# Values and output gate of three of four token blocks as seven block products with sums kept in PSUM

## The chip, the cores and the metric

The kernel runs on one core of one Trainium2 chip. The metric is the device time of one execution in microseconds (us); lower is better. TensorE multiplies, VectorE and ScalarE work on elements, GpSimd does a power now and then, and SyncE (SP) issues the DMA transfers.

## What is computed

One decoder layer on 2048 tokens of width 1024, in fp32. The part that the change touches is the combined input projection and what hangs on it:

```python
n = rms_norm(h, norm1_w)
z = n @ w_in            # columns: queries 256, keys 256, values 512, low rank 16, output gate 512, spatial u 512, spatial v 512
# A: gated linear attention, 4 heads (key 64, value 128 wide), chunks of 64 tokens
S_t = diag(alpha_t) S_{t-1} + k_t^T v_t ;  o_t = q_t S_t
A = rms_norm(o, gla_norm_w) * silu(gate)
# B: spatial gating, chunks of 128 tokens
B = u * (tril(W_s) @ layer_norm(v) + b)
h = h + concat([A, B]) @ w_out
h = h + (silu(m @ w_ffn_gate) * (m @ w_ffn_up)) @ w_ffn_down     # m = rms_norm(h)
out = rms_norm(h)
```

## The kernel before

The tokens are worked off in four blocks of 512 (`NB`); in the text they are the first to the fourth block, in the code `blk` 0 to 3. A loop `s` over two pairs runs `mix` and `project` (output projection) for two blocks, then gate and up (`gate_up`) and the down-projection (`down`) for both. Gate, up and down already run as seven block products of Winograd's form, with sums of blocks of `w_d` that a background generator, `down_sums` (L322 to L337, 11 jobs), writes to the DRAM tensor `td` during the first two blocks.

Every fp32 product is three fp32r matmuls (`mm3`, L112 to L116): each operand is split into a high part that ScalarE copies (L94) and a low part that VectorE subtracts (L95), 12 significant bits each. A weight tile (`load_w`, L101) is a load of 512 KB to a `raw` buffer (3 of them), the copy `whi` and the subtraction `wlo` (4 pairs in flight).

```python
def split(hi, lo, src):
    nc.scalar.copy(hi, src)
    nc.vector.tensor_tensor(lo, src, f32(hi), ALU.subtract)
```

Work that is no dense product is written as generators. `start` puts one into a list, and `tick` runs one step of each; `tok_group`, `col_pair` and the others call `tick` after each weight tile's matmuls. `finish` runs a generator to its end. Within that written order a scheduler sets the order of each engine's instructions, and each engine works its own in order. PSUM has 8 banks, one per `ps` tile.

In `mix` (L342) a block goes through: the first half of the gating values with the low rank columns; the decay; keys; queries; values (`tok_group` over the 512 value columns: 4 tiles of 24 matmuls, drained by ScalarE, L438), from which four DMAs (L442) bring the values into the halves of `right` that other rows hold; `chunks()` (L446), started when the values are there, in four steps of two chunks each. A step is 16 matmuls for the states' increments (L453), 8 updates of the state on VectorE (L462), 16 matmuls for the scores (L469) and 2 masked copies (L473). It runs in the ticks of the second half of the gating values (L483) and of the output gate (L510: again 4 tiles of 24 matmuls, drained by `gate_done`, ScalarE's Silu and a scale on VectorE, L506 and L508). `sv_norm` (L486) is the layer norm of the gating values, with GpSimd's power in between. Then `attend` (L517) runs in the ticks of the spatial gate's products (`gate_pair` with two tiles of `su` each, L551 to L573).

Of the kernel before, what the change touches and what calls it, by code (L numbers as in the profile page):

```python
# [8 lines left out]
F32 = mybir.dt.float32  # L9
# [24 lines left out]
def hybrid_block(ctx, tc, x, norm1_w, w_in, w_gate_up, b_gate_up, gla_norm_w, sg_ln_w, sg_ln_b,  # L34
# [28 lines left out]
    # A generator emits one step at a time; tick() runs a step of each after a weight tile's products.  # L63
# [37 lines left out]
    def load_w(srcs, a, b):  # L101
        """srcs: DRAM views [P, a, ...], side by side; the two parts of [P, a, b] in SBUF."""
# [9 lines left out]
    def mm3(o, l, r, first, last):  # L112
        (lh, ll), (rh, rl) = l, r
        nc.tensor.matmul(o, lhsT=ll, rhs=rh, start=first, stop=False)  # L114
        nc.tensor.matmul(o, lhsT=lh, rhs=rl, start=False, stop=False)  # L115
        nc.tensor.matmul(o, lhsT=lh, rhs=rh, start=False, stop=last)  # L116

    def rsq(dst, ss, n, k):
        """dst = 1 / sqrt(ss / n + eps)"""
# [10 lines left out]
    class Act:  # L130
        """A transposed operand: nk row tiles of 128 by 512 tokens, two parts."""
# [10 lines left out]
        def row(self, k, n=1):  # L142
            """Row tiles k .. k+n-1, for all tokens."""
# [3 lines left out]
        def put(self, i, t, src):  # L147
            """Row tiles 4i .. 4i+3 of token tile t from PSUM."""
            s = slice(t * P, (t + 1) * P)
            split(self.hi[i][:, :, s], self.lo[i][:, :, s], src.rearrange("p (a b) -> p a b", b=P))  # L150

    def row_tiles(u):
        """Two units as four row tiles of D."""
# [37 lines left out]
    def tok_group(w, col_list, act, ks=2, order=None, outer=None, done=None, before=None, ws=None, hook=None, pre=None):  # L191
        """Token-major product: four PSUM tiles [128 tokens, n]."""
# [39 lines left out]
    def col_pair(ws, act, a=0, b=NB):  # L232
        """Transposed product: two PSUM tiles [128 columns, tokens a..b]."""
# [23 lines left out]
    # 0 where a chunk starts, 1 elsewhere: the prefix scan's carry  # L257
# [3 lines left out]
    # keep[j, i] = 1 where j <= i, in both halves of the rows  # L261
# [10 lines left out]
    bd = dram.tile([2, P, 4, NB], F32, name="bd")  # L272

    # the decay's up-projection: rows hi, hi, lo against the low-rank input's hi, lo, hi
# [9 lines left out]
    def constants():  # L284
# [9 lines left out]
        # spatial gating: masked, transposed weights and the two biases  # L294
# [27 lines left out]
    def down_sums():  # L322
# [672 lines left out]
```

## Time and profile before

| | |
|---|---|
| runs, us | 2015.26, 2015.6, 2017.57 |
| median, us | 2015.6 |
| span of the profiled execution, us | 2014.3 |
| TensorE busy, us | 1987.2 (99%) |
| VectorE busy, us | 1422.5 (71%) |
| ScalarE busy, us | 858.8 (43%) |
| DMA engines busy | 45.2% |

The times are of whole executions. The profile is of one execution more, taken by the hardware profiler; its own time is its span, from the first instruction to the last. L95 is line 95 of the kernel. An engine is busy while an instruction of it runs; matmuls are pipelined, so a matmul's duration overlaps that of the next, and what one costs is read from the distance of starts. The granted clock is TensorE's, as a share of the full 2.4 GHz.

### The profile page before, as it was taken

The page shows a single profiled execution, that of the slowest core. Times are in us where ns is not written, and L with a number is a line of the kernel's source. Part 1 is how long each engine was busy: PE and PEld are TensorE (multiplying, and loading weights), DVE is VectorE, ACT ScalarE, POOL GpSimd, SP SyncE. Part 2 cuts the span into 40 slices and gives each one's busy share as a digit, 9 for nine tenths or more (in the row PEclk, how much of TensorE's full clock was granted, in tenths as well). Part 3 has the DMA queues.
Part 4 walks back from the last instruction along what each step waited for, and adds up shares of the span by engine and source line. Part 5 has one row for each costly group of instructions (what it writes and reads, how often), then busy time and mean ns, then how long its engine had stood idle before and what let it go on. Part 6 is the DMA issues. An engine that isn't in the chain of part 4 may idle for free. (4 is left out here: it accounts for less than half of the span.)

```text
span 2014.3 us, 26324 instructions
## 1 busy us (share of the span) xinstructions
PE 1987.2 (99%) x9909; PEld 1659.1 (82%) x9909; DVE 1422.5 (71%) x2397; ACT 858.8 (43%) x1418; POOL 80.8 (4%) x102
## 2 busy tenths in 40 slices
PE   7999999999999999999999999999999999999998
PEld 6888888878888888888888888887888888888886
DVE  5676776798777777555776655658977877775466
ACT  4534635453333333433562535346433333334334
POOL 1011000000000000000100100100000000000000
PEclk9999999999999999999999999999999999999999
DMA  5646664323323324865754344323332332367555
GB/s 192 188 168 222 228 200 167 115 94 105 115 95 102 118 95 145 290 200 185 242 178 105 115 143 144 103 84 116 114 111 95 106 114 95 104 208 268 188 164 197
DMA packets 189790, 303.05 MB, mean 150 GB/s; under 512 B 14503, under 2 KB 93021, under 8 KB 188638
## 3 DMA queue, kind: packets, MB, share of 16 engines
q1 hardware_dynamic: 189662, 301.36, 45.2%
q8 instruction: 78, 1.28, 0.3%
q14 instruction: 50, 0.41, 0.1%
HBM read 224.25 MB, written 72.88 MB: 148 GB/s over the span
## 5 line engine op out<-in xcount | busy, mean ns | idle before, releaser
L94 ACT CAST whi<-raw 128x1024 fp32r<-128x1024 f32 (+3 forms) x191 | 192.0, 1006 | 403.3 <-PE ps L115 208.5
L95 DVE TENSOR_TENSOR wlo<-raw,whi 128x1024 fp32r<-128x1024 f32 (+3 forms) x191 | 221.9, 1168 | 150.1 <-ACT whi L94 144.1
L114 PE MATMUL ps<-whi,aop 128*128 128x512 f32 x552 | 215.1, 390 | 0.0
L116 PE MATMUL ps<-whi,aop 128*128 128x512 f32 x552 | 214.8, 389 | 0.0
L115 PE MATMUL ps<-wlo,aop 128*128 128x512 f32 x552 | 214.8, 389 | 0.0
L94 ACT CAST op<-sw 128x512 fp32r<-128x512 f32 x176 | 107.5, 621 | 184.5 <-DVE sw L634 159.6
L114 PE MATMUL ps<-whi,nTl 128*128 128x512 f32 (+2 forms) x512 | 177.4, 346 | 3.4 <-DVE nTl L95 3.4
L116 PE MATMUL ps<-whi,nTh 128*128 128x512 f32 (+2 forms) x512 | 174.4, 341 | 0.0
L115 PE MATMUL ps<-wlo,nTh 128*128 128x512 f32 (+2 forms) x512 | 174.3, 340 | 0.0
L95 DVE TENSOR_TENSOR aop<-raw,aop 128x1024 fp32r<-128x1024 f32 x84 | 95.3, 1135 | 97.5 <-ACT aop L94 97.3
L95 DVE TENSOR_TENSOR op<-sw,op 128x512 fp32r<-128x512 f32 x176 | 121.5, 692 | 43.0 <-ACT op L94 42.6
L94 ACT CAST aop<-raw 128x1024 fp32r<-128x1024 f32 x84 | 82.0, 979 | 136.6 <-DMA raw<-ad 135.1
L116 PEld LDWEIGHTS ps<-whi,aop 128*128 128x128 f32 x552 | 103.6, 188 | 21.6
L115 PEld LDWEIGHTS ps<-wlo,aop 128*128 128x128 f32 x552 | 103.6, 188 | 21.4
L114 PEld LDWEIGHTS ps<-whi,aop 128*128 128x128 f32 x552 | 103.6, 188 | 21.4
L659 ACT COPY p<-ps 128x512 f32<-128x512 f32 x88 | 51.5, 588 | 149.2 <-PE ps L116 143.6
L95 DVE TENSOR_TENSOR op<-raw,op 128x512 fp32r<-128x512 f32 x132 | 89.3, 693 | 31.0 <-ACT op L94 30.5
L114 PEld LDWEIGHTS ps<-whi,nTl 128*128 128x128 f32 x512 | 98.1, 192 | 14.5 <-ACT whi L94 3.5
L116 PEld LDWEIGHTS ps<-whi,nTh 128*128 128x128 f32 x512 | 98.1, 192 | 10.2
L115 PEld LDWEIGHTS ps<-wlo,nTh 128*128 128x128 f32 x512 | 98.2, 192 | 9.4
L114 PE MATMUL ps<-whi,mixTl 128*128 128x512 f32 x256 | 101.9, 398 | 1.4 <-DVE mixTl L95 1.2
L114 PE MATMUL ps<-nTh,wlo 128*128 128x512 f32 x256 | 101.8, 398 | 0.0
(229 smaller groups left out, 4712.4 us busy)
## 6 DMA issues: line engine op xcount, KB each, us to landing
raw<-in_w_in_dram SPq DMA_DIRECT2D x72, 512.0 KB, 3.9
raw<-ad SPq DMA_DIRECT2D x70, 512.0 KB, 3.9
raw<-in_w_ffn_gate_dram SPq DMA_DIRECT2D x44, 512.0 KB, 3.6
raw<-in_w_ffn_up_dram SPq DMA_DIRECT2D x44, 512.0 KB, 3.6
raw<-td SPq DMA_DIRECT2D x40, 512.0 KB, 3.9
ad<-cg SPq DMA_DIRECT2D x66, 256.0 KB, 2.0
ad<-cs SPq DMA_DIRECT2D x22, 768.0 KB, 3.6
raw<-in_w_out_dram SPq DMA_DIRECT2D x32, 512.0 KB, 3.8
```

Source lines behind the costliest of these rows:

```text
L94: nc.scalar.copy(hi, src)
L95: nc.vector.tensor_tensor(lo, src, f32(hi), ALU.subtract)
L114: nc.tensor.matmul(o, lhsT=ll, rhs=rh, start=first, stop=False)
L115: nc.tensor.matmul(o, lhsT=lh, rhs=rl, start=False, stop=False)
L116: nc.tensor.matmul(o, lhsT=lh, rhs=rh, start=False, stop=last)
L659: nc.scalar.copy(t[m], o)
```

## The change

For the second to the fourth block values and output gate are one product: 512 tokens x 1024 by 1024 x 1024 columns, quartered by halves of the tokens, of the inner dimension and of the columns (values, gate). It is done in seven block products of 256 x 512 by 512 x 512 (`pair_product`), each with two weight tiles of 12 matmuls, in the order 1, 2, 7, 6, 4, 5, 3. The running sums stay in three pairs of PSUM banks: products 1, 6, 5, 3 add into one, 7 and 4 into another. `drain` reads a sum after a product: 1, 2, 6 and 4 give the values, 7, 5 and 3 the gate.

Four left operands are sums of quarters of the block's normed tokens (`Halves`, made in ticks of the stages before the product), four right operands are sums of quarters of `w_in`, which `weight_sums` (formerly `down_sums`, now 15 jobs, each in place in one buffer) writes to the DRAM tensor `vd`. The second half of the gating values now comes ahead of the product, and the chunk steps start after product 4. `mix` also loads its block's x rows anew (`hx`) at the start of `attend`. The first block is as before.

```diff
+    class Halves:
...
+            a, b, c = spare
+            whole(a, 0, 0)
+            whole(b, 1, 0)
+            nc.vector.tensor_tensor(c, a, b, ALU.subtract)
+            put(7, c)
+            yield
+            whole(c, 1, 1)
+            nc.vector.tensor_tensor(c, c, b, ALU.add)
+            put(5, c)
+            yield
...
+    def pair_product(load, left, order, bank, drain):
+
+        acc = {}
+        for m in order:
+            key = bank[m]
+            first = key not in acc
+            if first:
+                acc[key] = [ps(), ps()]
+            for kk in range(2):
+                hi, lo = load(m, kk)
+                for th in range(2):
+                    for j in range(2):
+                        mm3(acc[key][th], left(m, 2 * kk + j, th), (hi[:, j, :], lo[:, j, :]),
+                            first and kk + j == 0, kk + j == 2, True)
+                    if kk:
+                        drain(m, th, acc[key][th])
+                tick()
...
-        for j in range(NF // 2):
-            raw, t = bigt(F32, "wdraw"), bigt(F32, "wdt")
...
+        jobs = [(blocks(w_in, (k, 4 + k), (C_V, C_GOUT)), vd[:, k]) for k in range(4)]
+        jobs += [(blocks(w_d, (2 * j, 2 * j + 1), (0, 512)), td[:, j]) for j in range(NF // 2)]
         for _ in range(8):
             yield
+        for srcs, dst in jobs:
+            t = bigt(F32, "wsum")
+            for i, src in enumerate(srcs):
+                nc.sync.dma_start(t[:, i], src)
+            b11, b12, b21, b22 = (t[:, i] for i in range(4))
+            nc.vector.tensor_tensor(b11, b12, b11, ALU.subtract)
+            nc.vector.tensor_tensor(b12, b22, b12, ALU.subtract)
+            nc.vector.tensor_tensor(b22, b22, b11, ALU.subtract)
+            nc.vector.tensor_tensor(b21, b21, b22, ALU.subtract)
+            nc.sync.dma_start(dst.rearrange("m p d -> p m d"), t)
             for _ in range(4):
                 yield
...
+        if halves is None:
+            tok_group(w_in, [(C_V, 512)], nT, done=lambda t, acc: nc.scalar.copy(v[:, t, :], acc))
+            g_chunks = chunks_start()
+            second_half()
...
+            tok_group(w_in, [(C_GOUT, 512)], nT, done=gate_done)
+        else:
+            second_half()
+            g_svn = start(sv_norm())
+            finish(g_half)
...
+            def drain(m, th, acc):
+                lo, hi = th, 2 + th
+                if m == 1:
+                    nc.scalar.copy(v[:, lo, :], acc)
+                elif m == 2:
+                    nc.vector.tensor_tensor(v[:, lo, :], acc, v[:, lo, :], ALU.add)
+                elif m == 7:
+                    nc.scalar.copy(gw[:, hi, :], acc)
+                elif m == 6:
+                    nc.scalar.copy(v[:, hi, :], acc)
+                elif m == 4:
+                    nc.vector.tensor_tensor(v[:, hi, :], acc, v[:, hi, :], ALU.add)
+                    if th:
+                        started.append(chunks_start())
+                elif m == 5:
+                    nc.vector.tensor_tensor(gw[:, hi, :], acc, gw[:, hi, :], ALU.add)
+                    nc.scalar.activation(gw[:, hi, :], gw[:, hi, :], AF.Silu)
+                    gate_scale(hi)
+                else:
+                    gate_done(lo, acc)
+
+            pair_product(load, halves, (1, 2, 7, 6, 4, 5, 3), {1: 0, 6: 0, 5: 0, 3: 0, 2: 1, 7: 2, 4: 2}, drain)
...
+        hx = dma_x(x2, blk)
```

Before, VectorE in the third block from the third chunk step to the second tile of the spatial gate (`rs`, `sv`: layer norm of the gating values; `wlo`: low part of a weight tile; `right`, `state`: the state's updates; `left`: the masked copy of the scores; `gw`: the gate's scale):

```order
L462 SCALAR_TENSOR_TENSOR right_8774<-right_8773,dec,ps 64x128 x4
L462 SCALAR_TENSOR_TENSOR right_8773<-right_8774,dec,ps 64x128 x4
L473 COPY_PREDICATED left<-keep,ps 64x2x128 x2
L120 TENSOR_SCALAR rs<-mv 128x4
L95 TENSOR_TENSOR wlo<-raw,whi 128x1024
L497 TENSOR_SCALAR sv<-sv,mv,rs 128x128 x4
L462 SCALAR_TENSOR_TENSOR right_8774<-right_8773,dec,ps 64x128 x4
L462 SCALAR_TENSOR_TENSOR state<-right_8774,dec,ps 64x128 x4
L473 COPY_PREDICATED left<-keep,ps 64x2x128 x2
L95 TENSOR_TENSOR wlo<-raw,whi 128x1024 x2
L508 TENSOR_TENSOR gw<-gw,gnw 128x512 x3
L95 TENSOR_TENSOR wlo<-raw,whi 128x1024
```

Between two chunk steps there is a weight split, and the spatial gate's first splits stand ahead of the gate's scales.

With the change, VectorE in the third block from the last values' adds (L620 behind product 4) into the third chunk step (L536 and L547 are the steps' updates and masked copies, L624 is the gate's add behind product 5, L581 its scale):

```order
L620 TENSOR_TENSOR v<-ps,v 128x512 x2
L95 TENSOR_TENSOR wlo<-raw,whi 128x1024
L536 SCALAR_TENSOR_TENSOR right_8900<-right_8899,dec,ps 64x128 x4
L536 SCALAR_TENSOR_TENSOR right_8899<-right_8900,dec,ps 64x128 x4
L547 COPY_PREDICATED left<-keep,ps 64x2x128 x2
L536 SCALAR_TENSOR_TENSOR right_8900<-right_8899,dec,ps 64x128 x4
L536 SCALAR_TENSOR_TENSOR right_8899<-right_8900,dec,ps 64x128 x4
L547 COPY_PREDICATED left<-keep,ps 64x2x128 x2
L624 TENSOR_TENSOR gw<-ps,gw 128x512 x2
L536 SCALAR_TENSOR_TENSOR right_8900<-right_8899,dec,ps 64x128 x4
L536 SCALAR_TENSOR_TENSOR right_8899<-right_8900,dec,ps 64x128
L581 TENSOR_TENSOR gw<-gw,gnw 128x512 x2
```

The one split here is that of product 3's second tile; the first two steps stand one behind the other. The same queue goes on, to the spatial gate:

```order
L536 SCALAR_TENSOR_TENSOR right_8899<-right_8900,dec,ps 64x128 x3
L547 COPY_PREDICATED left<-keep,ps 64x2x128 x2
L536 SCALAR_TENSOR_TENSOR right_8900<-right_8899,dec,ps 64x128 x4
L536 SCALAR_TENSOR_TENSOR state<-right_8900,dec,ps 64x128 x4
L547 COPY_PREDICATED left<-keep,ps 64x2x128 x2
L581 TENSOR_TENSOR gw<-gw,gnw 128x512 x2
L95 TENSOR_TENSOR wlo<-raw,whi 128x1024 x5
```

The split of the spatial gate's first tile is the first of the last five, behind all steps and the scales of product 3's gate. In the fourth block the rows are the same.

With the change, VectorE in the second block, the end of the third chunk step to the spatial gate's splits (`wsum`: the weight sums):

```order
L536 SCALAR_TENSOR_TENSOR right_2240<-right_2241,dec,ps 64x128
L547 COPY_PREDICATED left<-keep,ps 64x2x128 x2
L536 SCALAR_TENSOR_TENSOR right_2241<-right_2240,dec,ps 64x128 x4
L536 SCALAR_TENSOR_TENSOR state<-right_2241,dec,ps 64x128 x4
L547 COPY_PREDICATED left<-keep,ps 64x2x128 x2
L95 TENSOR_TENSOR wlo<-raw,whi 128x1024
L403 TENSOR_TENSOR wsum<-wsum 128x512
L404 TENSOR_TENSOR wsum<-wsum 128x512
L405 TENSOR_TENSOR wsum<-wsum 128x512
L406 TENSOR_TENSOR wsum<-wsum 128x512
L581 TENSOR_TENSOR gw<-gw,gnw 128x512 x2
L95 TENSOR_TENSOR wlo<-raw,whi 128x1024 x5
```

Here the split of product 3's second tile stands behind the fourth step, and a job of the weight sums ahead of the gate's scales; the four subtractions of another job stand among the third step's updates.

## Rows read from the trace of the kernel before

**Rows 1.** The page's first part: busy us (share of the span) x instructions of each engine.
```profile
PE 1987.2 (99%) x9909; PEld 1659.1 (82%) x9909; DVE 1422.5 (71%) x2397; ACT 858.8 (43%) x1418; POOL 80.8 (4%) x102
```
**Rows 2.** TensorE's waits: us in total, times, longest us.
```profile
PE ps L453 <- DVE right L462: 1.2, 3, 0.4
```
**Rows 3.** Stretches: busy us of PE, PEld, DVE, ACT, POOL, clock, DMA share, GB/s.
```profile
202.00:241.00 39.00, 39.00 (x234) 34.81 (x233) 25.75 (x61) 24.96 (x40) 4.36 (x5) 1.00 0.62 212
241.00:275.00 34.00, 34.00 (x224) 29.97 (x223) 23.98 (x42) 14.95 (x21) 0.00 (x0) 1.00 0.84 267
275.00:298.00 23.00, 22.50 (x180) 18.21 (x179) 19.73 (x65) 3.92 (x5) 4.04 (x4) 1.00 0.53 173
5.00:10.00 5.00, 0.20 (x1) 0.20 (x2) 1.64 (x4) 3.15 (x5) 0.65 (x2) 1.00 1.02 402
34.00:37.00 3.00, 3.00 (x15) 3.00 (x15) 0.76 (x4) 1.05 (x1) 0.00 (x0) 0.50 0.00 0
```
**Rows 4.** Timeline of TensorE, 59.5 to 62.9 us: start, us, instruction.
```profile
59.69 0.39 PE L115 MATMUL ps<-nTl,whi 128*128 128x512 f32 x1
...
62.86 0.39 PE L114 MATMUL ps<-whi,nTl 128*128 128x512 f32 x1
```
**Rows 5.** Timeline of VectorE in the fourth block; in brackets the idle time before.
```profile
1262.39 3.00 DVE L462 SCALAR_TENSOR_TENSOR right<-right,dec,ps 64x128 f32<-64x128 f32 x8 [4.68 <-PE ps L453]
1265.30 0.92 DVE L473 COPY_PREDICATED left<-keep,ps 64x256 f32<-64x256 int32 x2
1266.12 1.20 DVE L95 TENSOR_TENSOR wlo<-raw,whi 128x1024 fp32r<-128x1024 f32 x1
1267.25 0.47 DVE L492 BATCH_NORM_STATS2 bst<-sv 128x6 f32<-128x128 f32 x2
...
1269.51 1.12 DVE L497 TENSOR_SCALAR sv<-sv,mv,rs 128x128 f32<-128x128 f32 x4 [1.05 <-POOL rs L121]
...
1287.22 1.48 DVE L462 SCALAR_TENSOR_TENSOR right<-right,dec,ps 64x128 f32<-64x128 f32 x4
```
**Rows 6.** ScalarE's groups: busy us, mean ns of one, idle before.
```profile
L94 ACT CAST whi<-raw 128x1024 fp32r<-128x1024 f32 x167 | 174.9, 1049 | 353.5 <-PE ps L115 171.0 <-PE ps L114 59.2 <-DMA raw<-td 32.9
L506 ACT ACTIVATE gw<-ps 128x512 f32<-128x512 f32 x16 | 9.3, 596 | 2.3 <-PE ps L116 2.3
L506 ACT ACT_TABLE_LOAD x4 | 5.1, 1283 | 0.1
```
**Rows 7.** Timeline of VectorE in the second block, sums of w_d and a split.
```profile
264.28 0.69 DVE L333 TENSOR_TENSOR wdt<-wdraw 128x512 f32<-128x512 f32 x1
264.88 0.69 DVE L334 TENSOR_TENSOR wdt<-wdraw,wdt 128x512 f32<-128x512 f32 x1
265.49 1.22 DVE L95 TENSOR_TENSOR wlo<-raw,whi 128x1024 fp32r<-128x1024 f32 x1
```
**Rows 8.** Timeline of TensorE, a chunk step in the fourth block.
```profile
1261.69 0.68 PE L453 MATMUL ps<-v,eu 64*64 64x128 f32 x16
...
1262.76 0.39 PE L114 MATMUL ps<-whi,nTl 128*128 128x256 f32 x1
```
**Rows 9.** Timeline of TensorE, the fourth chunk step of the fourth block.
```profile
1283.33 0.55 PE L453 MATMUL ps<-v,eu 64*64 64x128 f32 x6 [0.43 <-DVE right L462]
```
**Rows 10.** The page's DMA issues: KB each, median us from issue to landing.
```profile
raw<-in_w_in_dram SPq DMA_DIRECT2D x72, 512.0 KB, 3.9
```
**Rows 11.** Timeline of TensorE, 33 to 38.2 us.
```profile
33.16 0.48 PE L319 MATMUL ps<-bs_bc,ones 1*128 1x128 f32 x2
...
34.22 0.43 PE L116 MATMUL ps<-whi,nTh 128*128 128x272 f32 x1
...
36.04 0.43 PE L115 MATMUL ps<-wlo,nTh 128*128 128x272 f32 x1
...
37.27 0.29 PE L115 MATMUL ps<-wlo,nTh 128*128 128x272 f32 x1
...
38.15 0.29 PE L116 MATMUL ps<-whi,nTh 128*128 128x272 f32 x1
```

More of the change, by code (lines that the diff above doesn't have):

```diff
@@ L110, in load_w, with mm3 @@
         return hi, lo
[L112 removed]
+    def mm3(o, l, r, first, last, shared=False):
         (lh, ll), (rh, rl) = l, r
[L114 to L116 removed]
+        nc.tensor.matmul(o, lhsT=ll, rhs=rh, start=first, stop=False, skip_group_check=shared)
+        nc.tensor.matmul(o, lhsT=lh, rhs=rl, start=False, stop=False, skip_group_check=shared)
+        nc.tensor.matmul(o, lhsT=lh, rhs=rh, start=False, stop=last, skip_group_check=shared)
     def rsq(dst, ss, n, k):
@@ L150, in put, with __init__, make, whole @@
             split(self.hi[i][:, :, s], self.lo[i][:, :, s], src.rearrange("p (a b) -> p a b", b=P))
+    class Halves:
+        def __init__(self, act):
+            self.act, self.sums = act, {}
+        def make(self):
+            act = self.act
+            u = bigt(F32, "hs").rearrange("p a b -> p (a b)")
+            spare = [u[:, i * D:(i + 1) * D].rearrange("p (a b) -> p a b", a=4) for i in range(2)]
+            spare.append(nwp.tile([P, D], F32, name="nw", tag="nw").rearrange("p (a b) -> p a b", a=4))
+            def whole(dst, th, kh):
+                s = slice(th * 256, th * 256 + 256)
+                nc.vector.tensor_tensor(dst, f32(act.hi[kh][:, :, s]), f32(act.lo[kh][:, :, s]), ALU.add)
+            def put(m, src):
+                o = bigt(F32R, "hop").rearrange("p a b -> p (a b)")
+                h, l = (o[:, i * D:(i + 1) * D].rearrange("p (a b) -> p a b", a=4) for i in range(2))
+                split(h, l, src)
+                self.sums[m] = h, l
+            a, b, c = spare
[8 more added lines that the diff above has]
+            yield
+            nc.vector.tensor_tensor(c, c, a, ALU.subtract)
+            put(6, c)
+            yield
+            whole(b, 0, 1)
+            nc.vector.tensor_tensor(b, b, c, ALU.subtract)
+            put(3, b)
+        def __call__(self, m, k, th):
+            if m in self.sums:
+                return tuple(x[:, k, th * P:(th + 1) * P] for x in self.sums[m])
+            kh, t = {1: (0, 0), 2: (1, 0), 4: (1, 2)}[m]
+            return self.act(4 * kh + k, (t + th) * P, (t + th + 1) * P)
@@ L272, in hybrid_block @@
     bd = dram.tile([2, P, 4, NB], F32, name="bd")
+    vd = dram.tile([4, 4, P, 512], F32, name="vd")
     LR = 96
@@ L339, in hybrid_block @@
     start(constants())
-    start(down_sums())
+    start(weight_sums())
     def mix(blk, nT, first_w):
         sv = bigt(F32, "sv")
+        halves = Halves(nT) if blk else None
+        g_half = start(halves.make()) if blk else None
         glrT = tp.tile([LR, NB], F32R, name="glrT", tag="tp")
@@ L476, in chunks, with chunks_start, second_half @@
                 yield
-        for hh in range(2):
-            nc.scalar.copy(right(0)[mine(hh), hh], state[mine(hh)])
-        g_chunks = start(chunks())
-        tok_group(w_in, [(C_SV + 256, 256)], nT, ks=4,
-                  done=lambda t, acc: nc.scalar.activation(sv[:, t, 256:512], acc[:, :256], AF.Gelu))
+        def chunks_start():
+            values_put()
+            finish(g_kend)
+            for hh in range(2):
+                nc.scalar.copy(right(0)[mine(hh), hh], state[mine(hh)])
+            return start(chunks())
+        def second_half():
+            tok_group(w_in, [(C_SV + 256, 256)], nT, ks=4,
+                      done=lambda t, acc: nc.scalar.activation(sv[:, t, 256:512], acc[:, :256], AF.Gelu))
         def sv_norm():
```

55 lines of the change are left out of this document (29 added, 26 removed).

## The prediction

> Blocks are counted from one to four. Lines 614, 620, 624, 581 (values, gate and its scale), 536 and 547 (chunk step) and 403 to 406 (weight sums) are those of the changed kernel, as in the order pieces above; all others are those of the kernel before.
>
> **What bounds the kernel now.** I read the engines' busy shares first: TensorE is busy 99% of the span, VectorE 71% [rows 1]. TensorE's waits come next: for the chunk steps, which this change moves, it waits 1.2 us in all [rows 2]. So the span is TensorE's count of matmuls, and any matmul that goes is gained as long as nobody makes TensorE wait. The third view is the table by stretches for the second block: TensorE is full, and VectorE has the least to spare, 25.75 of 39 us before the values, 23.98 of 34 us in values and second half, 19.73 of 23 us in the output gate, where TensorE first loses half a microsecond [rows 3]. The question is what VectorE must do in a shorter stage.
>
> **What is removed.** Values and gate take 8 weight tiles of 24 matmuls; now 14 tiles of 12. That is 24 matmuls fewer per block, 72 in all. A matmul's duration (0.39) is not its price: 14 matmuls after the first row of the group the next one starts 3.17 us later, 0.2264 each [rows 4]. So 5.43 us per block, **16.3 us** in all, and a tile of 12 lasts 2.72 us. The Trainium skill ("TensorE: Matmul & The Clock Gate", Part 1, "Wait — 56ns, not 53.3ns?") gives 215.7 ns from start to start for 512 columns at the full clock; by that the gain would be 15.5 us. The trace's pitch is 5% longer, so the row stands.
>
> **What is added before the product.** Per block VectorE makes 12 operations of 1024 columns (8 sums, 4 low parts) and ScalarE 4 copies. After a 1024-column split the next instruction starts 1.13 us later [rows 5], so 13.6 us of VectorE; in the 39 us ahead of the values 13.25 are free and 10 more in the next 34 [rows 3]. ScalarE has 14 of 39 us free for 4 times 1.05 [rows 3, 6]. I cost this at nothing: the cover is VectorE's idle time ahead of a stage in which a tile lasts over 5 us. Without cover the 0.4 us by which it overruns the first stages would be lost in each block. The weight sums have four more jobs of four subtractions, 0.61 us apart [rows 7]: 9.7 us, in the second block and what follows it. The extra transfers (2 MB per job in and out, 2 MB of x rows per block) meet 212 GB/s in the first stages, where 402 were moved once [rows 3]. Price 0 to 2 us; I take 0.5.
>
> **What is moved: the chunk steps.** Before, the second half and the output gate covered them, one step per tile of 24 matmuls or more. In the fourth block the first step starts on VectorE at 1262.39 and the fourth at 1287.22, 8.3 us apart on average, and before the first VectorE had idled 4.68 us [rows 5]. One step is 8 updates and 2 masked copies and holds VectorE from 1262.39 to 1266.12, 3.73 us [rows 5]; on TensorE it runs from 1261.69 to 1262.76, 1.07 us [rows 8]. Now the steps start only when product 4 is summed, since they need all values, and come one per tile of 12: VectorE needs 3.73 us where TensorE's tile and step last 2.72 + 1.07 = 3.79. That alone just fits, but the same tail has more for VectorE.
>
> In the third and fourth block, from the end of product 4, its queue holds (second and third order piece) the last add into the values 0.61, a split 1.13, four steps 14.92, two adds into the gate 1.21, four gate scales 2.42 [rows 5, 7], and then the split of the first tile of the spatial gate, 1.22 [rows 7]: 21.5 us. TensorE has four tiles and four steps, 10.87 + 4.28 = 15.15 us, and then needs that split. VectorE works in order, so **TensorE waits 6.4 us** per block: 0.4 at the second step's scores, whose bank the first step's updates free (the trace has such a wait of 0.43 already [rows 9]), about 1 at product 3, whose first matmul needs the bank that the gate add reads, 0.8 at the last step's scores, and 4.2 at the spatial gate. Against 5.43 gained, each of these blocks loses 1.0 us. Bounds: 4.0 us if the first add and split and half of a pair's scales were done beside product 4; 8.3 us if a Silu and its table, 0.60 and 1.28 [rows 6], fell on the chain.
>
> In the second block the weight sums of w_d still run. Eight of their subtractions stand in the same tail (last order piece), 4.84 us, and the split of product 3's second tile stands behind the last step instead of ahead of the first. By the same count that split ends 22.7 us after product 4; product 3's second tile lasts until 25.4, its Silu and two scales until 27.3, the spatial gate's split until 28.5. TensorE's own work is 15.15: a wait of 13.3 us. Earlier, at product 6, a split stands behind four subtractions, 2.42, and behind the normalisation's scale, which waits for GpSimd for 1.05 us [rows 5]; walking the queue against 2.72 us a tile gives 2.7 us (0 at best, 5 at worst). Together **16.0 us**, net a loss of 10.6. The spatial gate's first tile also has two jobs' loads, a store and x rows ahead of it on SP's queue, about 6 MB; at the 267 to 402 GB/s of rows 3 these take 15 to 22 us, to which the 3.9 us of a load's own landing come [rows 10], and the 28 us hide nearly all. I put no more on it; the upper bound is 4 us.
>
> **The sum.** -16.3 + 6.4 + 6.4 + 16.0 + 0.5 = +13.0 us. The profiled execution's span is 2014.3, 1.3 below the median of the three runs, 2015.6; what lies around the span is not touched, so I add to the median: **2028.6 us**.
>
> **Rivals.**
> *The queue keeps up (faster).* If VectorE's list is worked off while TensorE still has tiles, the whole 16.3 us go: 1999.3. The point that decides is 20.6 us from product 4's end to the spatial gate's first split (15.15 plus the 5.43 gained): below it a block gains. For it: the third and fourth blocks' list is only 0.9 us above that point, and in 275 to 298 VectorE was 86% busy with TensorE losing 0.5 us [rows 3]. Against: the second block's list is 8 us above, and its queue is in order. With waits of 3.2 in the third and fourth block and 5 in the second the time is 2011. Chance 0.22, over 1999 to 2011.
> *The second block behaves like the other two.* If its subtractions find gaps, three waits of 6.4 stand against 16.3, plus 0.5: +3.4, 2019.0; range 2012 to 2022. For it: VectorE idles at times in the products before the tail, and the slack there may be larger than I counted. Against: the order of the tail. Chance 0.20, of which 0.14 within 0.2%.
> *The clock falls (slower still).* From 34 to 37 us the granted clock was 0.50, the lower level of 1.2 GHz [rows 3], after small matmuls on one row (0.48 us for two of 128 columns), and 8 matmuls of 272 columns took 1.82 us from start to start, 0.227 each; at the full clock 7 took 0.88, 0.126 each [rows 11]. The 15 of that stretch lost 1.5 us. Three tails with chunk steps and a long wait could each do the same: 4.5 us, 2033.1, and with the late load in the second block 2037. The same page of the Trainium skill (Part 1, "What's actually happening") says that the half rate is the default and activity lifts it, a rule against any change that trades matmuls for pauses; the trace agrees at 34 us (0.50), and shows 1.00 in all stretches of the second block [rows 3]. Chance 0.13, 2034 to 2045.
> *It does not do what it says:* the number of matmuls is fixed by the program, so this has no chance.
>
> **How the numbers follow.** My own case, 2022 to 2034, has 0.45. Below 2011.6 is faster by over 0.2% (4 us, about what runs of this kernel can tell from no change): 0.22. Within: 0.14. Above 2019.6: 0.45 + 0.13 + 0.06 = 0.64. The range of 2003 to 2038 leaves out about 0.10 below, most of the full gain, and 0.07 above.
>
> **What would show it.** Right: 72 matmuls of 512 columns less; TensorE's waits list a VectorE split (wlo) of about 4 us twice and one near 10 us once, at the first matmul of the spatial gate; VectorE is busy without a gap from product 4 to that split. Wrong: no wait over 2 us there, or waits in the first stages for the halves (hop), or for raw loads (a DMA as releaser), or a granted clock of 0.50 in the tails. If VectorE's list lasts under 20.6 us in the third block, the step that fails is the 3.73 us per chunk step.

## The result, and the profile after

The changed kernel takes 2049.2 us (median of 4 runs, 2048.64 to 2050.96) against 2016.6 for the kernel before on the same chip (2015.26 to 2018.05): ratio 1.0162, 95% interval 1.0148 to 1.0177. It is slower, as forecast, but by 32.6 us and not by 13.0; the time lies above the range. What a place in the kernel gains or loses is read from one profiled execution, which can lie away from the median of its runs (2037.3 us against 2042.3 in the first experiment, 2040.4 against 2046.6 in the third, 2019.5 against 2015.4 in the sixth run).

The page's first part after the change, against [rows 1]:

```profile
PE 1987.0 (97%) x9837; PEld 1652.4 (81%) x9837; DVE 1503.1 (73%) x2485; ACT 892.6 (44%) x1454; POOL 88.5 (4%) x102
```

72 matmuls fewer, and yet TensorE is busy as long as before. Its waits, against [rows 2] (us in total, times, longest):

```profile
PE ps L115 <- DVE wlo L95: 15.0, 4, 4.8
...
PE ps L116 <- DVE wlo L95: 9.2, 4, 4.9
PE ps L543 <- DVE right L536: 5.0, 5, 2.5
...
PE ps L115 <- DVE gw L624: 1.6, 3, 0.5
```

TensorE now waits for weight splits, as the forecast said, but more often and in more places. TensorE's waits in the second block's product (timeline of TensorE; in brackets the idle time and what ended it):

```profile
272.66 0.50 PE L116 MATMUL ps<-wlo,hop 128*128 128x512 f32 x1 [3.19 <-DVE wlo L95]
...
291.12 0.67 PE L543 MATMUL ps<-left,eu 64*64 64x64 f32 x14 [1.17 <-DVE right L536]
...
303.49 0.67 PE L543 MATMUL ps<-left,eu 64*64 64x64 f32 x8 [2.47 <-DVE right L536]
309.07 0.80 PE L116 MATMUL ps<-wlo,hop 128*128 128x512 f32 x1 [4.92 <-DVE wlo L95]
316.68 0.76 PE L115 MATMUL ps<-nTh,wlo 128*128 128x512 f32 x1 [2.97 <-DVE wlo L95]
```

The first is product 6, the others are the tail; one more of 0.91 us is at product 7's first tile, and one of 0.53 at product 3. From 290 to 310 us VectorE is busy 19.1 of 20 us, so the tail's waits up to there are for its queue and not for loads. The columns of [rows 3] again, for stretches after the change:

```profile
275.00:280.00 5.00, 5.00 (x18) 3.97 (x18) 1.41 (x2) 1.72 (x3) 0.00 (x0) 0.76 0.98 318
...
305.00:320.00 15.00, 7.96 (x18) 5.82 (x19) 9.64 (x17) 3.22 (x5) 0.00 (x0) 0.50 1.03 345
...
1050.00:1060.00 10.00, 7.29 (x27) 5.90 (x28) 10.00 (x19) 8.00 (x11) 0.00 (x0) 0.83 0.51 147
1135.00:1140.00 5.00, 1.41 (x5) 0.92 (x4) 4.91 (x9) 2.48 (x3) 0.00 (x0) 0.76 0.01 2
1140.00:1145.00 5.00, 5.00 (x14) 3.86 (x14) 2.38 (x3) 1.04 (x1) 0.00 (x0) 0.56 0.92 278
...
1325.00:1330.00 5.00, 5.00 (x16) 3.92 (x15) 1.23 (x1) 1.05 (x1) 0.00 (x0) 0.63 0.75 260
```

Where [rows 3] have a clock of 1.00 in all stretches of the second block, 305 to 320 us now has 0.50, the level of 1.2 GHz, with TensorE busy 8 of 15 us. Behind the long waits of this execution (3.19 us at product 6, 3.60 ahead of the spatial gate) the clock is down for some microseconds, and matmuls that run then take longer: in 1140 to 1145 TensorE was busy all five microseconds at 0.56, so 5 x 0.44 = 2.2 of them were lost. This is why the busy time did not fall.

**Where the 33 us lie.** I took the start of the same TensorE instruction in both traces, place by place; the difference grows or shrinks only where something happened.

| part of the program | change, us | of what |
|---|---|---|
| first block | -1.7 | arises among the start-up's loads, before 40 us; with the same code there the fourth and fifth run have -0.1 and +0.4 |
| second block up to the product | 0.0 | halves hidden |
| second block's product to the transposing of the attention's result (323.58 before, 339.78 after) | +17.9 | matmuls -5.4, waits +16.3, low clock +7.0 |
| its projection, first products of gate and up | +2.8 | waits for splits (1.2 and 0.4 longest; the kernel before has one of 1.6 there), low clock behind them (about 1.5); last weight sums at 406 to 411 us |
| third block, first stage | +6.5 | a wait of 4.8, the rest low clock |
| third block's product and tail | +2.1 | -5.4, waits +4.9, low clock +2.6 |
| fourth block's product and tail | +2.2 | -5.4, waits +4.8, low clock +2.8 |
| last down-projection | +3.8 | open |
| sum | +33.6 | spans: 2047.6 - 2014.3 = 33.3 |

Low clock is what is left of a row after matmuls and waits. Busy time x (1 - granted clock), summed over the stretches of 5 us, gives 6.4, 2.5 and 2.6 for the three, so the remainder is nearly accounted for. The last row varies between kernels that don't touch that part (0.0 to +5.1 in the first four experiments), so I don't put it down to the change.

**The tail of the third block**, VectorE, which [rows 5, 7] forecast:

```profile
1116.63 1.28 DVE L620 TENSOR_TENSOR v<-ps,v 128x512 f32<-128x512 f32 x2
1118.12 1.23 DVE L95 TENSOR_TENSOR wlo<-raw,whi 128x1024 fp32r<-128x1024 f32 x1 [0.21 <-ACT whi L94]
1119.26 3.00 DVE L536 SCALAR_TENSOR_TENSOR right<-right,dec,ps 64x128 f32<-64x128 f32 x8
1122.17 0.91 DVE L547 COPY_PREDICATED left<-keep,ps 64x256 f32<-64x256 int32 x2
1122.99 2.99 DVE L536 SCALAR_TENSOR_TENSOR right<-right,dec,ps 64x128 f32<-64x128 f32 x8
...
1136.56 1.28 DVE L581 TENSOR_TENSOR gw<-gw,gnw 128x512 f32<-128x512 f32 x2
1137.76 2.35 DVE L95 TENSOR_TENSOR wlo<-raw,whi 128x1024 fp32r<-128x1024 f32 x2
```

and TensorE's first matmul of the spatial gate:

```profile
1139.12 0.77 PE L115 MATMUL ps<-nTh,wlo 128*128 128x512 f32 x1 [3.60 <-DVE wlo L95]
```

VectorE has one gap (0.21) from product 4 to that split. From the first chunk step (1116.86 on TensorE) to the split's end, 1138.98, it takes 22.1 us; 21.5 was forecast. A chunk step holds it 1122.99 - 1119.26 = 3.73 us, as before.

**The first stage of the third block**, VectorE and then TensorE (L934 is the final norm of the first pair's output, L168 and L183 make the halves; L95 is the split that the keys wait for):

```profile
1045.57 2.74 DVE L934 SCALAR_TENSOR_TENSOR hx<-hx,st,nw 128x512 f32<-128x512 f32 x4 [0.44 <-POOL st L122]
1048.22 1.22 DVE L168 TENSOR_TENSOR nw<-nTh,nTl 128x1024 f32<-128x1024 f32 x1
...
1049.51 1.22 DVE L183 TENSOR_TENSOR nw<-nw,hs 128x1024 f32<-128x1024 f32 x1
...
1051.44 1.21 DVE L95 TENSOR_TENSOR wlo<-raw,whi 128x1024 fp32r<-128x1024 f32 x1
```

```profile
1052.70 0.79 PE L115 MATMUL ps<-nTh,wlo 128*128 128x512 f32 x1 [4.82 <-DVE wlo L95]
```

Here VectorE still norms the output of the first pair of blocks, and the halves stand ahead of the split.

### The profile page after: what moved, and what is told of

Same layout as the page of the kernel before. It is cut to its first block, busy times and chain, and to the rows that moved or that the text cites. A ratio compares the mean times of both kernels' runs of the same rounds, so it can differ in the third digit from the quotient of the medians.

```text
span 2047.6 us, 26475 instructions
## 1 busy us (share of the span) xinstructions
PE 1987.0 (97%) x9837; PEld 1652.4 (81%) x9837; DVE 1503.1 (73%) x2485; ACT 892.6 (44%) x1454; POOL 88.5 (4%) x102
## 5 line engine op out<-in xcount | busy, mean ns | idle before, releaser
L94 ACT CAST whi<-raw 128x1024 fp32r<-128x1024 f32 (+2 forms) x209 | 210.6, 1010 | 350.0 <-PE ps L116 131.8
L95 DVE TENSOR_TENSOR wlo<-raw,whi 128x1024 fp32r<-128x1024 f32 (+2 forms) x209 | 243.2, 1171 | 141.0 <-ACT whi L94 130.0
L95 DVE TENSOR_TENSOR aop<-raw,aop 128x1024 fp32r<-128x1024 f32 x84 | 95.2, 1134 | 96.4 <-ACT aop L94 96.0
L95 DVE TENSOR_TENSOR op<-sw,op 128x512 fp32r<-128x512 f32 x176 | 120.6, 687 | 42.8 <-ACT op L94 42.3
L115 PE MATMUL ps<-whi,nTl 128*128 128x512 f32 (+2 forms) x392 | 128.4, 328 | 3.4 <-DVE nTl L95 3.4
L116 PE MATMUL ps<-wlo,nTh 128*128 128x512 f32 (+2 forms) x392 | 126.6, 323 | 0.2 <-DVE wlo L95 0.2
L117 PE MATMUL ps<-whi,nTh 128*128 128x512 f32 (+2 forms) x392 | 126.6, 323 | 0.0
L115 PE MATMUL ps<-nTh,wlo 128*128 128x512 f32 x256 | 106.1, 415 | 15.0 <-DVE wlo L95 15.0
L95 DVE TENSOR_TENSOR op<-raw,op 128x512 fp32r<-128x512 f32 x132 | 88.8, 687 | 31.5 <-ACT op L94 31.0
L122 POOL TENSOR_TENSOR st<-st,half 128x1 f32<-128x1 f32 x48 | 41.6, 875 | 1471.4 <-DVE st L121 1444.8
L116 PE MATMUL ps<-nTl,whi 128*128 128x512 f32 x256 | 103.4, 404 | 0.0
L117 PE MATMUL ps<-nTh,whi 128*128 128x512 f32 x256 | 103.2, 403 | 0.0
```

The costliest lines, as they stand in the source:

```text
L117: nc.tensor.matmul(o, lhsT=lh, rhs=rh, start=False, stop=last, skip_group_check=shared)
L122: nc.gpsimd.tensor_tensor(dst, dst, half[:, :k], ALU.pow)
```

## The experiments

My theory after the result: three things cost, each a queue in order: the tail (a list of VectorE's longer than TensorE's work), the weight sums in the second block's tail, and the halves in the third block's first stage; the low clock follows the waits. Rivals: the transfers, or the clock as a cause of its own.

**1. Weight sums twice as fast**

```diff
-            for _ in range(4):
+            for _ in range(2):
                 yield
```

> Weight sums at double pace (a job every 2 ticks instead of 4), so that all 15 jobs are done before the second block's product; nothing is left out. Theory (the second block loses more than the other two because eight subtractions stand in VectorE's queue in its product): its tail becomes like the third block's, 4.9 us of waits instead of 16.3 and less of the 7 us at the low clock, and the first products of gate and up lose their 2.8 us: 11 to 16 us faster than the changed kernel, 2033 to 2038. Rival (the second block's waits come from late loads, since most transfers run there): they stay, 2045 or more.

Measured: 2042.3 us, ratio 1.0136 (1.0119 to 1.0153), between the theory's range and the rival's. In the profiled execution the second block's product costs +4.6 in place of +17.9: in place of the five waits above stand 3.6 us at the spatial gate, 1.8 at product 6, 1.1 at a step, and two of 0.5 to 0.6. So 13 us of that block hung on the sums. The 2.8 us at the start of gate and up are gone (0.0), so these hung on the sums too. But the first block loses 4.3 us from the end of its start-up on (a wait of 3.6 for a split): the work that was pulled forward costs there. The third block's first stage loses 9.8 where it had 6.5; the sums are done by then, and the fourth run, which changes nothing up to there, has 8.9, so I don't put this down to the pace.

**2. No halves**

```diff
-            kh, t = {1: (0, 0), 2: (1, 0), 4: (1, 2)}[m]
+            kh, t = {1: (0, 0), 2: (1, 0), 4: (1, 2), 7: (0, 0), 6: (1, 0), 5: (0, 2), 3: (0, 2)}[m]
...
-        g_half = start(halves.make()) if blk else None
+        g_half = None
```

> Leaves out the sums of the left operand: the four products that take sums of token quarters take plain quarters instead, so 12 VectorE operations and 4 ScalarE copies per block are gone; the matmuls, the weight sums and the order of the products stay. Theory (in the third block these operations stand with the final norm of the first pair ahead of the keys' first split): the wait of 4.8 us there and its 1.7 us at the low clock go, all else stays: 6.5 us faster than the changed kernel, about 2043. Rival (they also fill VectorE's queue into the product): more than 10 us faster. Rival (the final norm alone makes that wait): no change, 2049.

Measured: 2030.4 us, ratio 1.0081 (1.0062 to 1.0100): 15.9 us over the kernel before on the same chip, where the change has 32.6. That is the rival of more than 10 us, not the theory's 6.5. The third block's first stage is at 0.0 in place of +6.5, so the final norm alone makes no wait; it takes the halves. The second block's product is at +11.1 in place of +17.9, although the first stages, where the halves are made, lost nothing there in either. TensorE's longest wait in it is now this one:

```profile
308.54 0.80 PE L116 MATMUL ps<-wlo,nTh 128*128 128x512 f32 x1 [6.35 <-DVE wlo L95]
```

The two profiled executions differ by 18.7 us: 6.5 and 6.8 of it in these two places, the rest in the two tails (0.0 and +1.2 here, +2.1 and +2.2 with the halves) and the last down-projection. Of the 6.8 us, 5.2 are waits (11.1 in place of 16.3) and the rest low clock. How halves made early cost this in the product behind is not shown. The weight sums' subtractions are not what they push back: the tail's two jobs start at 298.9 and 308.4 us without the halves and at 299.1 and 309.0 with them. What differs is that the waits at products 7 and 6 (0.9 and 3.2) shrink to four of 0.5 to 0.8 in the products before the tail, and that the spatial gate's first split (309.0) now stands among the last job's subtractions and not behind them, so that the wait of 3.0 there is gone.

The tails' waits stay (3.5 and 3.6 us), as the theory of the queue has it. But the low clock does not always follow them. The third block's first matmul of the spatial gate, and the stretch around it, without the halves:

```profile
1126.35 0.47 PE L115 MATMUL ps<-nTh,wlo 128*128 128x512 f32 x1 [3.52 <-DVE wlo L95]
```

```profile
1125.00:1130.00 5.00, 3.65 (x16) 3.10 (x17) 3.47 (x4) 0.34 (x1) 0.00 (x0) 1.00 0.49 131
```

The wait is as long as in the changed kernel (3.60) and the clock stays at 1.00: this is the 2 us by which the tail is better here, and not the halves. The first experiment's wait of 3.60 us in the first block also has 1.00 behind it. What decides whether the clock falls behind a wait of this length is not shown by any run here.

**3. Second half of the gating values behind the product**

```diff
-            second_half()
-            g_svn = start(sv_norm())
             finish(g_half)
...
             pair_product(load, halves, (1, 2, 7, 6, 4, 5, 3), {1: 0, 6: 0, 5: 0, 3: 0, 2: 1, 7: 2, 4: 2}, drain)
+            second_half()
+            g_svn = start(sv_norm())
```

> The second half of the gating values and its layer norm go back behind the block product (in the second to the fourth block), so that 11.6 us more of matmuls follow the product's tail; nothing is left out. Theory of the queue (what hurts is that the next stage's first split stands behind all four chunk steps and the gate's scales): it does so here too, now the second half's, so each tail keeps its wait of 3.5 to 5 us, and the time stays within 4 us of the changed kernel, 2045 to 2053. Rival, theory of the amount (TensorE has too little work beside VectorE's 21.5 us): the 11.6 us cover it, the waits and the low clock behind them go in three blocks: 2025 to 2035.

Measured: 2046.6 us, ratio 1.0150 (1.0132 to 1.0168), as the theory of the queue has it. A wait of 3.0 us for a split follows product 3 in the third and fourth block, where it was 3.6 (the two places cost +0.6 and -0.9). In the third:

```profile
1123.09 0.38 PE L116 MATMUL ps<-wlo,nTh 128*128 128x256 f32 x1 [3.01 <-DVE wlo L95]
```

Other work for TensorE behind the product needs a split too, and that stands behind the same list. So the order of VectorE's queue sets the wait, and not a lack of work for TensorE. The second block's product costs +12.5 here.

**4. Useless matmuls in the pause**

```diff
+        for _ in range(fill):
+            nc.tensor.matmul(acc[0][0], lhsT=left(1, 0, 0)[0], rhs=hi[:, 0, :], start=True, stop=True)
...
-            pair_product(load, halves, (1, 2, 7, 6, 4, 5, 3), {1: 0, 6: 0, 5: 0, 3: 0, 2: 1, 7: 2, 4: 2}, drain)
+            pair_product(load, halves, (1, 2, 7, 6, 4, 5, 3), {1: 0, 6: 0, 5: 0, 3: 0, 2: 1, 7: 2, 4: 2}, drain, 16 if blk > 1 else 0)
```

> In the third and fourth block 16 useless matmuls of 512 columns (3.6 us) are put between the product's last matmul and the spatial gate's first, into a PSUM bank that has been read; all else is computed as before. Theory of the clock (half a wait's price is that the clock falls in it): the 16 fit into the waits of 3.6 and 4.8 us, the granted clock stays at 1.00 there, and the kernel gets faster by doing more: 2.5 us per block, 2044. Rival (the slow matmuls behind the wait have another cause, such as loads or PSUM): no gain, the low clock stays, 2048 to 2052.

Measured: 2046.1 us, ratio 1.0153 (1.0138 to 1.0169). Stretches, as above:

```profile
1140.00:1145.00 5.00, 5.00 (x23) 3.87 (x22) 4.97 (x8) 2.44 (x3) 0.00 (x0) 1.00 0.10 10
...
1325.00:1330.00 5.00, 5.00 (x23) 4.14 (x23) 2.46 (x3) 1.05 (x1) 0.00 (x0) 1.00 0.76 220
```

The time lies between the theory's 2044 and the rival's 2048, and its interval overlaps that of the changed kernel (1.0148 to 1.0177), so the whole time alone does not show a gain; the two places do. The clock is 1.00 where it was 0.56 and 0.63. From the first chunk step to the attention's first matmul (L657) the third block takes 28.0 us for 30.4, the fourth 28.2 for 30.6: 2.3 and 2.4 us won each by giving TensorE 16 matmuls more. That shows the price of the clock in these two tails by itself, beside that of the wait. The Trainium skill ("TensorE: Matmul & The Clock Gate", Part 1, "What's actually happening") calls the throttled state the default, which activity lifts; the trace agrees with that here (0.56 and 0.63 behind a pause, 1.00 with the pause filled).

**5. Chunk steps at half the pace.** The generator yields twice per step, and its rest runs beside the spatial gate.

```diff
+                if blk:
+                    yield
...
-        finish(g_chunks)
+        if not (blk):
+            finish(g_chunks)
```

> The changed kernel with the chunk steps in every second tick from product 4 on (two weight tiles between two steps), so that the last step falls into the spatial gate's products; nothing is left out. Theory of the queue: with two tiles per step (5.4 + 1.1 us on TensorE against 3.7 on VectorE) the splits stand between the steps, the waits of 3.6 us ahead of the spatial gate and the low clock behind them go in the third and fourth block (from +2.1 and +2.2 us against the kernel before to about -4 each), and the second block loses 4 to 8 us less: 2026 to 2036. Rival of the amount: the wait only moves on, to the output projection's wait for the attention's rows, and the time stays above 2042.

Measured: 2038.0 us, ratio 1.0114 (1.0099 to 1.0129), above the theory's range and below the rival's. The third block's product gains 5.8 and the fourth's 6.0, the whole of what 24 matmuls are worth. VectorE in the third block now:

```profile
1128.98 2.99 DVE L536 SCALAR_TENSOR_TENSOR right<-right,dec,ps 64x128 f32<-64x128 f32 x8
1131.89 0.92 DVE L547 COPY_PREDICATED left<-keep,ps 64x256 f32<-64x256 int32 x2
1132.70 1.21 DVE L95 TENSOR_TENSOR wlo<-raw,whi 128x1024 fp32r<-128x1024 f32 x1
```

A split follows the step, where another step followed before. The second block became worse, +23.1, by one wait; TensorE, and then SP's queue:

```profile
322.52 0.77 PE L115 MATMUL ps<-nTh,wlo 128*128 128x512 f32 x1 [18.44 <-DVE wlo L95]
```

```profile
306.69 4.17 SPq L407 DMA_DIRECT2D td<-wsum  x2
310.95 1.53 SPq L239 DMA_DIRECT2D hx<-in_x_dram  x2
312.58 2.52 SPq L106 DMA_DIRECT2D raw<-in_w_in_dram  x3
```

The spatial gate's load stands behind two stores of weight sums, which wait for VectorE's subtractions (the last one at 309.76), and behind x rows; VectorE then idles 8.4 us until that load has landed and ScalarE has made its copy (at 320.07). So the 18.4 us are made of the stores' waits, the x rows and some 7 us until the load has landed.

**6 to 9. Which blocks, which engine, which pace.** Four versions with the halved pace. In the sixth and seventh only the third and fourth block have the product (`blk > 1` in place of `blk`), the sums of `w_d` come first, and the third block's halves start 3 ticks later; the seventh makes the halves' sums (L168) on GpSimd:

```diff
-        jobs = [(blocks(w_in, (k, 4 + k), (C_V, C_GOUT)), vd[:, k]) for k in range(4)]
-        jobs += [(blocks(w_d, (2 * j, 2 * j + 1), (0, 512)), td[:, j]) for j in range(NF // 2)]
+        jobs = [(blocks(w_d, (2 * j, 2 * j + 1), (0, 512)), td[:, j]) for j in range(NF // 2)]
+        jobs += [(blocks(w_in, (k, 4 + k), (C_V, C_GOUT)), vd[:, k]) for k in range(4)]
...
-        halves = Halves(nT) if blk else None
-        g_half = start(halves.make()) if blk else None
+        halves = Halves(nT) if blk > 1 else None
+        g_half = start(halves.make(3 if blk == 2 else 0)) if blk > 1 else None
...
-                nc.vector.tensor_tensor(dst, f32(act.hi[kh][:, :, s]), f32(act.lo[kh][:, :, s]), ALU.add)
+                nc.gpsimd.tensor_tensor(dst, f32(act.hi[kh][:, :, s]), f32(act.lo[kh][:, :, s]), ALU.add)
```

The eighth has all three blocks, with GpSimd; the ninth the third and fourth alone, without GpSimd, halves 2 ticks later, the old order of jobs, one every 3 ticks.

> The block product in the third and fourth block alone, steps spread as in the run before; the sums of w_in come last among the weight sums, since the third block is the first to read them; in the third block the halves start three ticks later, behind the first pair's final norm. Nothing is left out. Theory (the second block's loss is the weight sums and halves beside its product, the third's is halves beside the final norm): the second block costs nothing, the wait of 4.8 us in the third's first stage goes, third and fourth gain about 4 us each, and the late weight sums give back 1 to 3 us at the start of gate and up: 2004 to 2012, faster than the kernel before (2014.5 in these runs). Rival (halves cost VectorE's time wherever they stand): the third block's stall only moves to keys or queries, 2013 to 2020.

> As the run before, but the four whole quarters (high part plus low part, 1024 columns each) are added on GpSimd, so VectorE makes 8 operations of 1024 columns per block instead of 12. Theory (VectorE's queue is what costs): where waits on it are left ahead of the product they go, 0 to 4 us faster than the run before. Rival (GpSimd is too slow or slows VectorE beside it; no trace here shows an addition of this size on it): the product waits for its halves, 1 to 10 us slower.

> All three blocks with the block product, steps spread, the halves of the third block three ticks later, the whole quarters on GpSimd; the weight sums as in the changed kernel. Theory: against the run with the steps spread alone, the third block's 6.5 us and some 2 to 5 us of the second block go: 2016 to 2026. What is left over the kernel before is the weight sums in the second block's product. Rival (the second block's loss has another cause than the queue): no more than 6.5 us, 2024 or more.

> The block product in the third and fourth block alone with the chunk steps in every second tick, the halves of the third block two ticks later, and a weight-sum job in every third tick, so that all 15 are done with the second block's spatial gate; nothing is left out. Theory (the gain of 5.4 us a block is there once VectorE's queue is clear, and the rest of the run before with these two blocks was lost to weight sums that ran into gate, up and down): third and fourth block gain 5 to 6 us each, the denser sums cost up to 4 us in the first two blocks: 2005 to 2011 where the kernel before takes 2015. Rival (VectorE is full in the first two blocks as well, so the sums cost there what they cost later): 2012 to 2018.

| run | us | ratio (interval) | where it loses or gains against before, us |
|---|---|---|---|
| 6 | 2015.4 | 1.0000 (0.9991 to 1.0010) | third -1.2, fourth -6.3; first pair's gate and up +4.2, down-projection +4.7 |
| 7 | 2019.9 | 1.0023 (1.0014 to 1.0032) | third's first stage +1.2, product +0.3; fourth's first stage +1.9, product -6.3; gate, up and down of the first pair +4.5 |
| 8 | 2030.2 | 1.0071 (1.0054 to 1.0088) | second +3.2 and +9.5, third's first stage +1.3, product +0.7; fourth's first stage +1.9, product -6.4 |
| 9 | 2014.3 | 0.9996 (0.9987 to 1.0005) | first +4.8, third -2.9, fourth -4.4 |

All four missed the theory's ranges, and all four times lie in their rivals'. The fourth block's product gains 6.3 to 6.4 us in three of them and 4.4 in run 9. Without the product in the second block the loss of that block is gone. Losses stand where the weight sums now lie: in the first pair's down-projection where they come late, in the first block where they come early; that the sums cause them is read from the place alone. And the third block gains 1.2 us or less in runs 6 to 8 and 2.9 in run 9, where it gained 5.8 in the fifth. With its halves made later its first stage is free in runs 6 and 9 (0.0), but waits for splits now stand in its product, in run 6 the longest at

```profile
1083.79 0.50 PE L116 MATMUL ps<-wlo,nTh 128*128 128x512 f32 x1 [1.76 <-DVE wlo L95]
```

So the rival of run 6 is right: the halves' cost moves on with them. GpSimd doesn't help: one such sum takes it 2.4 us or more where VectorE takes 1.2, and both runs with it lose 1.9 us in the fourth block's first stage, those without it nothing.

**10 to 12. All three blocks, the pace of the sums.** All have the halved pace of chunk steps and the third block's halves 2 ticks later. Run 10 has a job every 2 ticks; 11 and 12 have the old pace for the first three jobs and then 2, or 1 and 2 in turn:

```diff
-            for _ in range(4):
+            for _ in range(4 if n < 3 else 2):
                 yield
```

> All three blocks with the block product, steps in every second tick, the halves of the third block two ticks later, and a weight-sum job in every second tick, so that the sums are done ahead of the second block's product. Nothing is left out. Theory: second block about even (its product gains 5.4 us and its halves cost VectorE's 13.6 us beside the last sums), third and fourth gain 5 to 6 us each, the first block loses about 4 us as in the run with the faster sums alone: 2006 to 2014. Rival (the loads ahead of the spatial gate's first tile on SP's queue hold the second block as in the run with the steps spread alone, 18 us): 2020 or more.

> All three blocks' products, chunk steps spread over both yields, and the weight sums at the change's own pace (4 ticks) for the first three jobs, then every 2 ticks. If the first block's 6.8 us that the pace of 2 cost (a wait of 3.6 us and half clock between 110 and 130 us, where the DMA engines were 99% busy) come from the crowding of the transfers there, that block is about -1.7 us against the kernel before, the rest stays as with a pace of 2 throughout, and the time is about 2008 us. If VectorE's order is at fault, not the transfers, the loss moves to another place of the first two blocks and the time stays near 2014.5 us.

> As the run before, but after the third job the jobs come every 1 and 2 ticks in turn, so that the last one ends before the second block's product. If what is left of the sums in that product's tail costs, this is 2 to 5 us faster than the run before (about 2006 us); if the crowding of the transfers is what counts, the loss comes back in the end of the first block and the time is 2012 to 2016 us.

Run 10: 2014.6 us, ratio 0.9991 (0.9981 to 1.0001): level with the kernel before on its chip, where the change as it was lost 32.6 us, and just above the forecast range. The second block's product now gains 2.6, the third's 1.7, the fourth's 6.0; the first block loses 6.8 from the end of its start-up on. There the stretches are

```profile
90.00:110.00 20.00, 19.82 (x176) 16.66 (x176) 17.09 (x49) 3.53 (x6) 1.39 (x1) 1.00 0.99 306
110.00:130.00 20.00, 16.39 (x72) 13.02 (x69) 17.20 (x46) 5.57 (x7) 4.51 (x3) 0.83 0.62 217
```

with the DMA engines full up to 110 us and a wait of 3.6 us behind. Run 11 (2026.9 us, 1.0047, 1.0035 to 1.0059) missed my expectation of 2008: the first block, counted in the same way, is indeed at -0.8 where it had +6.8, but the second block's product is at +16.1. SP's queue, ScalarE and TensorE there:

```profile
255.09 4.01 SPq L409 DMA_DIRECT2D td<-wsum  x2
259.15 3.18 SPq L403 DMA_DIRECT2D wsum<-in_w_ffn_down_dram  x4
262.38 0.51 SPq L106 DMA_DIRECT2D raw<-in_w_in_dram  x1
```

```profile
268.02 1.05 ACT L94 CAST whi<-raw 128x1024 fp32r<-128x1024 f32 x1 [8.97 <-DMA raw<-in_w_in_dram]
```

```profile
269.12 1.22 PE L115 MATMUL ps<-whi,nTl 128*128 128x512 f32 x2 [4.98 <-ACT whi L94]
```

A weight load stands behind two stores that wait for VectorE and behind four loads of the sums, and lands 5.6 us after its issue in place of 3.9 [rows 10]. Run 12 (2019.0 us, 1.0007, 0.9998 to 1.0016) missed both of its forecasts. It has the loss in the second block's first stage: +6.3, with a wait of 3.4 for the rows that VectorE scales there (`xsu`). VectorE and then TensorE there:

```profile
204.35 1.23 DVE L168 TENSOR_TENSOR hs<-nTh,nTl 128x1024 f32<-128x1024 f32 x1
205.50 2.47 DVE L227 SCALAR_TENSOR_TENSOR xsu<-hx,st,nw 128x1024 f32<-128x1024 f32 x2
```

```profile
206.83 0.69 PE L234 MATMUL ps<-ident,xsu 128*128 128x128 f32 x2 [3.41 <-DVE xsu L227]
```

What stands ahead of these rows is not the sums but the halves (L168 makes a part of them, and so do the two operations ahead of it). So here the halves cost in the second block's first stage, where they cost nothing in the changed kernel. No pace of the three beats the kernel before by more than can be measured; each moves a cost to another stage.

## Why the prediction was wrong in size

**The matmuls, -16.3.** Held: 9909 - 9837 = 72 fewer, and where a product runs free (fifth run) the third and fourth block gain 5.8 and 6.0, near the 5.43 forecast.

**The tails, 6.4 each.** The walk of VectorE's queue was right (22.1 us measured, 21.5 forecast, waits at the four places named). TensorE's own four tiles and steps took 17.3 us (22.26 from 1116.86 to 1139.12, less 4.95 of waits) and not 15.15, so the waits are 4.9 and 4.8. A part of that is the step: from the last matmul ahead of it to the second behind it (1116.54 to 1118.26), less two matmuls, it costs 1.27 us and not 1.07. The term was too large by 1.5 and 1.6: without the clock a tail wins 5.4 - 4.9 = 0.5 us, where a loss of 1.0 was forecast.

**The second block, 16.0.** Measured 16.3 us of waits in the product: 3.2 at product 6 (2.7 forecast), 0.9 at product 7 (not forecast), and 12.0 in the tail (13.3 forecast). The first experiment shows the weight sums to be most of it. That the sum came so near is luck in part: the second experiment shows that 6.8 us of this block's loss, 5.2 of them waits, go with the halves, which were costed at nothing.

**The step that failed first: the clock.** It stood as a rival, 1.5 us per tail, at a chance of 0.13, and not in the sum; its range, 2034 to 2045, ends below the measured time too. It came in all three tails: 7.0, 2.6 and 2.8 us, 12.4 in sum, and a further 1.7 and about 1.5 in the rows of the halves and of the jobs. The rival's price came from one stretch of 3 us behind matmuls on one row; behind the waits of 3.6 us it was 2.3 to 2.4 (fourth experiment), and nothing behind one of 3.52 (second experiment). A forecast of long waits had to carry it in the sum, as a range. Its evidence against, a clock of 1.00 in all stretches of the second block [rows 3], came from stretches without a wait over 0.5 us.

**The step that failed second: "I cost this at nothing".** The cover was read from the second block and taken for all three. It held in the second block's first stages (0.0), and failed in the third's: there VectorE has the first pair's final norm in the same stage, 6.5 us lost, low clock included. Run 12 shows that it need not hold in the second block either (+6.3). The bound of 0.4 us per block was worked out from a stage that lacks that work. The forecast named "waits in the first stages for the halves" among what would show it wrong, and gave them no price; the wait that came is for a weight split that stands behind the halves.

**Extra jobs and loads, 0.5.** Up to gate and up 2.8 us are lost where the last jobs now lie (406 to 411 us; in the kernel before the last subtraction was at 309.6), and they go when the sums are done earlier (first experiment). The last 3.8 us, in the final down-projection, stay open as to their cause.

So 13.0 + 12.4 (clock) + 6.5 (halves) + 2.3 (jobs) + 3.8 (end) - 2.8 (shorter waits: 1.5, 1.6, less 0.3 more in the second block) - 1.7 (first block) = 33.5, against 33.3. The rival that the second block behaves like the others did not come, nor the one that the queue keeps up: for both, VectorE's list had to be shorter than it was.

## What to carry to other kernels

Cover is read in the stage of each block where the work is to lie, not in one block for all: the third block's first stage had a job the second had not. Making it later moved the wait to a later stage. A forecast of a wait of some microseconds on TensorE has to allow for the low clock behind it, here from nothing (second experiment) to 2.3 and 2.4 us (fourth experiment) for a wait of 3.5 to 3.6 us. And work that is put on VectorE in the background is charged twice, at the engine and at the queue of stores and loads behind it: in the fifth run and in run 11 weight loads stood on SP's queue behind stores that waited for VectorE, and TensorE waited for them.

## What the runs showed of the hardware

That filling a pause with useless matmuls is faster than waiting was not expected at this size: 16 more matmuls, 2.3 us less from the first chunk step to the attention's first matmul. Nor was it that the same wait, 3.52 us against 3.60, can leave the clock at 1.00. That stores that wait on SP's queue, with the loads behind them, can grow to a wait of 18.4 us on TensorE (fifth run) was not expected either: I had put 4 us as the upper bound of that, for the changed kernel, where it held.
